# Feature-major products split into two 64-row halves of the array, each half with its own PSUM bank

## The chip, the cores and the metric

The kernel runs on one core of one Trainium2 chip. The core has TensorE (PE, matmuls; PEld, its weight loads), VectorE (DVE), ScalarE (ACT), GpSimd (POOL), and SyncE (SP), whose queue issues most transfers. The metric is the device time of one execution in microseconds, as the median of several runs; lower is better. The median of three runs of the kernel before is 3139.31 us.

## The reference, cut to what matters

Two transformer layers and then one hybrid layer over 256 tokens of width 2048, all in float32. Only two places of it are touched. In each of the two layers the projection of the SSD mixer goes through a causal convolution:

```python
h = rms_norm(x, attn_norm_g[l])
proj = h @ w_in[l]
xbc = jax.nn.silu(causal_depthwise_conv(xbc, conv_w, conv_b))   # xbc: 1536 columns of proj
```

In the hybrid layer two gates of 1024 columns each are taken from the input projection and multiply the outputs of the two attention branches:

```python
ya = (oa * jax.nn.silu(za)) @ w_br_a
yb = (ob * jax.nn.silu(zb)) @ w_br_b
```

The other matmuls (projections, attention, memory attention, the FFN of width 5632) stay as they are.

## The kernel before, in words

Activations and weights are float32, split into a high part that fits the `fp32r` format and a remainder. Each product is three fp32r matmuls, high times high, high times low, low times high, summed in PSUM. Weights come from memory in tiles of 512 KB: SP issues the transfer, ACT writes the high part `wh` (L411), DVE the remainder `wl` (L412). There are five buffers for raw tiles and four for split ones. These three steps have a raised priority, so that they stand early in their engines' orders. The order on PE is the order in which the program is written; on the other engines a scheduler fixes it when the kernel is built, and each engine runs its list in order.

`block` (L414 and on) makes outputs with tokens on the partitions: 512 columns in two PSUM banks, its matmuls being L423, L424 and L425. `block_fm` (L451) makes an output block with features on the partitions, 128 features by 256 tokens: 16 steps over the 2048 inputs, in each of them three matmuls of 128 rows, 128 columns of weights and 256 moving columns (L461, L462, L463), all into one tile of the PSUM pool `psw`. This pool has four banks and serves `block` too.

`block_fm` has two callers. `ssd_conv` calls it 12 times in each of two layers: DVE multiplies the block out of PSUM by the row scale `rb` (L798) into `u`, does the convolution over four taps (L801, L803 three times), ACT takes a tanh (L805) and DVE combines (L806). The tiles `u`, `g` and `th` come from the pool `k1` of six buffers (`t1`). `gate_fm` calls it four times, and is itself called four times in the hybrid layer: ACT takes a tanh out of PSUM (L1303), DVE combines it with the block out of PSUM (L1304). That makes 24 + 16 = 40 blocks.

Between matmuls the program calls `tick()`, which lets waiting tasks emit a step: transposes of earlier results (L377), parts of the attention of other heads (L654 to L670, L1502, L1507), and so on. So the matmuls of such tasks stand between those of a block, in an order that is fixed when the kernel is built. The attention scores of branch A (`scores`, L670) are float32 products of 64 rows, one head on rows 0 to 63, the other on rows 64 to 127, one after the other; a float32 product is two records in the trace.

`early()` raises the priority of what is emitted in it as the weights' steps have it. `HALVES` is `(slice(0, 64), slice(64, 128))`.

Of the kernel before, what the change touches and what calls it, by code (L numbers as in the profile page):

```python
# [14 lines left out]
AF = mybir.ActivationFunctionType  # L15
OP = mybir.AluOpType
# [3 lines left out]
P = 128  # L20
S = 256
# [211 lines left out]
class _Net:  # L233
# [216 lines left out]

    def block_fm(self, pairs, src):  # L451

        nc = self.nc
        pt = self.wbank([P, S])
        for hf in range(2):
            h, l = self.weights(src[hf], 8, P)
            for j in range(8):
                k = hf * 8 + j
                pairs[k // 4] = xh, xl = self.get(pairs[k // 4])
                c = k % 4  # L460
                nc.tensor.matmul(pt, lhsT=h[:, j], rhs=xh[:, c], start=(k == 0), stop=False)  # L461
                nc.tensor.matmul(pt, lhsT=h[:, j], rhs=xl[:, c], start=False, stop=False)  # L462
                nc.tensor.matmul(pt, lhsT=l[:, j], rhs=xh[:, c], start=False, stop=(k == 15))  # L463
                if k in (3, 7, 11):
                    self.tick()
        return pt

# [319 lines left out]
    def ssd_conv(self, l, pairs, rb):  # L789
        nc, I = self.nc, self.I  # L790
        cw = self.small([P, 60], name="cw", bufs=1)
        nc.vector.tensor_scalar(cw, self.p(f"{l}.conv"), 0.5, None, op0=OP.mult)
        cb = [self.slot([P, 4, S], "cb") for _ in range(3)]
        for c in range(12):
            pt = self.block_fm(pairs, I["w_in_x"][l, c])
            u = self.t1([P, 3 + S])
            nc.gpsimd.memset(u[:, 0:3], 0.0)
            nc.vector.tensor_tensor(u[:, 3:], pt, rb, op=OP.mult)  # L798
            w = lambda i: cw[:, c * 5 + i:c * 5 + i + 1]
            g = self.t1([P, S])  # L800
            nc.vector.tensor_scalar(g, u[:, 0:S], w(0), w(4), op0=OP.mult, op1=OP.add)  # L801
            for i in (1, 2, 3):
                nc.vector.scalar_tensor_tensor(g, u[:, i:i + S], w(i), g, op0=OP.mult, op1=OP.add)  # L803
            th = self.t1([P, S])
            nc.scalar.activation(th, g, AF.Tanh)  # L805
            nc.vector.scalar_tensor_tensor(cb[c // 4][:, c % 4], th, 1.0, g, op0=OP.add, op1=OP.mult)  # L806
            if c < 11:
                self.tick()
        return cb
# [486 lines left out]
    def gate_fm(self, pairs, src):  # L1296

        nc = self.nc
        out = self.slot([P, 4, S], "zf")
        for c in range(4):  # L1300
            pt = self.block_fm(pairs, src[c])
            th = self.t1([P, S])
            nc.scalar.activation(th, pt, AF.Tanh, scale=0.5)  # L1303
            nc.vector.scalar_tensor_tensor(out[:, c], th, 1.0, pt, op0=OP.add, op1=OP.mult)  # L1304
            self.tick()
        return out

# [383 lines left out]
```

## Time and profile before

| what | value |
|---|---|
| median of the runs | 3139.31 us (3138.55 to 3139.89, 3 runs) |
| the profiled execution's own time | 3138.04 us |
| its span, first to last instruction | 3136.0 us |
| PE busy | 3114.7 us, 99% |
| DVE busy | 2030.4 us, 65% |
| ACT busy | 1548.2 us, 49% |
| POOL busy | 52.6 us, 2% |
| mean granted TensorE clock | 0.998 of 2.4 GHz |

Busy time of PE counts from the start of a matmul to its modelled end. Matmuls overlap, so the time that one takes of the engine is read from the distance between starts, not from its duration.

### The profile page before, as it was taken

The numbers are of one execution on the slowest core, as the hardware profiler recorded it, in microseconds if no ns is written. First come the engines' busy times: TensorE is split into PE (matmuls) and PEld (weight loads), VectorE is DVE, ScalarE is ACT, GpSimd is POOL, SyncE is SP. The second block draws the span as 40 slices with busy tenths as digits, with TensorE's granted clock in tenths as the row PEclk, the third lists the DMA queues.
The fourth block names the chain that finished last, engine by engine and source line by source line (L and its number), as shares of the span: only waits on it lengthen the run. The fifth ranks groups of instructions, "written<-read, shape, count | busy, mean of one in ns | idle before, by whom it ended". The sixth has DMA issues, their size and how long they took to land.

```text
span 3136.0 us, 42057 instructions
## 1 busy us (share of the span) xinstructions
PE 3114.7 (99%) x15977; PEld 2619.4 (84%) x15977; DVE 2030.4 (65%) x3013; ACT 1548.2 (49%) x2187; POOL 52.6 (2%) x79
## 2 busy tenths in 40 slices
PE   9999999999999999999999999999999999999998
PEld 8988888888888889988888888888878888888887
DVE  6886665555555566886667667777666566455555
ACT  7475564444444455475664444444454456444443
POOL 0010000000000000010000000000000000000000
PEclk9999999999999999999999999999999999999999
DMA  8545555555555555554558777777765543555454
GB/s 299 177 165 168 188 168 188 191 192 191 192 188 192 190 188 177 170 182 151 202 193 288 251 256 273 270 255 260 253 220 191 184 145 123 194 181 182 162 183 152
DMA packets 175162, 625.31 MB, mean 199 GB/s; under 512 B 19696, under 2 KB 19952, under 8 KB 174704
## 3 DMA queue, kind: packets, MB, share of 16 engines
q1 hardware_dynamic: 173952, 620.26, 58.0%
q8 instruction: 125, 2.05, 0.3%
q10 hardware_dynamic: 1008, 2.37, 0.2%
q14 instruction: 77, 0.63, 0.1%
HBM read 620.46 MB, written 2.10 MB: 199 GB/s over the span
## 4 chain that ended last, share of the span: by engine, by line
PE 96%; DVE 1%; DMA 1%; issue 1%; ACT 0%; POOL 0%; SPq 0%; DVEq 0%; POOLq 0%; ACTq 0%
PE pw L423 27%; PE pw L425 27%; PE pw L424 27%; PE pw L461 2%; PE pw L462 2%; PE pw L463 2%; PE mb L377 2%; PE mb L670 1%; DMA wada<-w_ada 0%; DVE wl L412 0%; PE mb L1507 0%; PE mb L909 0%; PE mb L1353 0%; PE mb L892 0%; PE mb L1162 0%
## 5 line engine op out<-in xcount | busy, mean ns | idle before, releaser
L412 DVE TENSOR_TENSOR wl<-raw,wh 128x1024 fp32r<-128x1024 f32 (+3 forms) x1069 | 1285.6, 1204 | 971.7 <-ACT wh L411 969.5
L411 ACT ACTIVATE wh<-raw 128x1024 fp32r<-128x1024 f32 (+3 forms) x1069 | 1114.3, 1043 | 1370.0 <-PE pw L425 1248.5
L423 PE MATMUL pw<-wh,xh 128*128 128x512 f32 (+2 forms) x3952 | 1552.0, 393 | 5.7 <-ACT wh L411 4.6
L425 PE MATMUL pw<-wh,xl 128*128 128x512 f32 (+2 forms) x3952 | 1524.5, 386 | 0.0
L424 PE MATMUL pw<-wl,xh 128*128 128x512 f32 (+2 forms) x3952 | 1523.3, 385 | 0.8 <-DVE wl L412 0.8
L423 PEld LDWEIGHTS pw<-wh,xh 128*128 128x128 f32 x3952 | 743.4, 188 | 151.0 <-ACT wh L411 5.7
L425 PEld LDWEIGHTS pw<-wh,xl 128*128 128x128 f32 x3952 | 742.5, 188 | 150.1 <-DVE xl L368 0.7
L424 PEld LDWEIGHTS pw<-wl,xh 128*128 128x128 f32 x3952 | 743.9, 188 | 142.1 <-DVE wl L412 2.2
L461 PE MATMUL pw<-xh,wh 128*128 128x256 f32 x640 | 183.0, 286 | 0.0
L463 PE MATMUL pw<-xh,wl 128*128 128x256 f32 x640 | 181.0, 283 | 0.0
L462 PE MATMUL pw<-xl,wh 128*128 128x256 f32 x640 | 181.0, 283 | 0.0
L485 DVE TENSOR_TENSOR x<-x,pw 128x512 f32<-128x512 f32 x224 | 145.0, 679 | 3.9 <-PE pw L425 3.9
L1245 DVE CUSTOM_DVE_ANT_0 wada<-wada,crow 128x1024 f32<-128x1024 f32 x96 | 117.3, 1222 | 39.6 <-DMA wada<-w_ada 39.4
L461 PEld LDWEIGHTS pw<-xh,wh 128*128 128x128 f32 x640 | 122.7, 192 | 0.8 <-issue 0.3
L462 PEld LDWEIGHTS pw<-xl,wh 128*128 128x128 f32 x640 | 122.7, 192 | 0.1
L463 PEld LDWEIGHTS pw<-xh,wl 128*128 128x128 f32 x640 | 122.7, 192 | 0.0
L630 ACT ACTIVATE t<-t,mn 128x256 f32<-128x256 f32 (+1 forms) x128 | 57.9, 453 | 44.5 <-DVE mn L627 42.5
L367 ACT ACTIVATE xh<-mb,par 128x256 fp32r<-128x256 f32 x112 | 50.9, 466 | 13.1 <-PE mb L377 12.2
L368 DVE SCALAR_TENSOR_TENSOR xl<-mb,par,xh 128x256 fp32r<-128x256 f32 x112 | 51.9, 478 | 4.0 <-ACT xh L367 2.8
L334 POOL TENSOR_TENSOR xr<-rs,mhalf 128x1 f32<-128x1 f32 x16 | 9.9, 621 | 2482.4 <-DVE rs L330 2278.9
L358 ACT ACTIVATE xh<-mb 128x512 fp32r<-128x512 f32 (+1 forms) x68 | 35.1, 517 | 31.1 <-PE mb L377 16.3
L359 DVE TENSOR_TENSOR xl<-mb,xh 128x512 fp32r<-128x512 f32 (+1 forms) x68 | 39.2, 591 | 4.3 <-ACT xh L358 3.9
(363 smaller groups left out, 1436.0 us busy)
## 6 DMA issues: line engine op xcount, KB each, us to landing
raw<-w_gate SPq DMA_DIRECT2D x176, 512.0 KB, 3.5
raw<-w_up SPq DMA_DIRECT2D x176, 512.0 KB, 3.5
raw<-w_down SPq DMA_DIRECT2D x176, 512.0 KB, 3.5
raw<-w_out SPq DMA_DIRECT2D x96, 512.0 KB, 3.4
wada<-w_ada SPq DMA_DIRECT2D x96, 512.0 KB, 5.6
raw<-w_in_x SPq DMA_DIRECT2D x48, 512.0 KB, 3.8
raw<-w_in_z SPq DMA_DIRECT2D x32, 512.0 KB, 3.5
raw<-w_ma SPq DMA_DIRECT2D x32, 512.0 KB, 3.2
```

Source lines behind the costliest of these rows:

```text
L377: self.nc.tensor.transpose(t[:, j, m * P:(m + 1) * P], src(m), self.ident)
L411: nc.scalar.activation(h, raw, AF.Copy)
L412: nc.vector.tensor_tensor(l, raw, h.bitcast(F32), op=OP.subtract)
L423: nc.tensor.matmul(pt[m], lhsT=xh[:, k, ms], rhs=wh[:, j], start=c == 0, stop=False)
L424: nc.tensor.matmul(pt[m], lhsT=xh[:, k, ms], rhs=wl[:, j], start=False, stop=False)
L425: nc.tensor.matmul(pt[m], lhsT=xl[:, k, ms], rhs=wh[:, j], start=False, stop=c == 4 * n - 1)
L461: nc.tensor.matmul(pt, lhsT=h[:, j], rhs=xh[:, c], start=(k == 0), stop=False)
L462: nc.tensor.matmul(pt, lhsT=h[:, j], rhs=xl[:, c], start=False, stop=False)
L463: nc.tensor.matmul(pt, lhsT=l[:, j], rhs=xh[:, c], start=False, stop=(k == 15))
L485: self.nc.vector.tensor_tensor(xs, xs, pt[m], op=OP.add)
L630: nc.scalar.activation(e[:, a:b], z[:, a:b], AF.Exp, scale=-1.0, bias=mn[:, m:m + 1], accum_out=su[:, m:m + 1])
L1245: nc.vector.tensor_tensor_reduce(out=t, in0=t, in1=self.crow[hf], scale=1.0, scalar=0.0, op0=OP.mult, op1=OP.add, accum_out=self.adap[:, j ...
```

## The change

In `block_fm` each of the three matmuls of a step becomes two, one over rows 0 to 63 of the weights and the moving data, one over rows 64 to 127. They alternate. The first of each two sums into one PSUM tile, the second into another; `block_fm` returns both. A new function `joined` copies the first tile to SBUF on ACT and adds the second to it on DVE, both in `early()`. In `ssd_conv` the multiplication by `rb` then goes from SBUF to SBUF, on POOL instead of DVE. In `gate_fm` the tanh and the combination read the joined block in SBUF instead of PSUM.

```diff
     def block_fm(self, pairs, src):
         nc = self.nc
-        pt = self.wbank([P, S])
+        pt = [self.wbank([P, S]) for _ in range(2)]
         for hf in range(2):
             h, l = self.weights(src[hf], 8, P)
             for j in range(8):
                 k = hf * 8 + j
                 pairs[k // 4] = xh, xl = self.get(pairs[k // 4])
                 c = k % 4
-                nc.tensor.matmul(pt, lhsT=h[:, j], rhs=xh[:, c], start=(k == 0), stop=False)
-                nc.tensor.matmul(pt, lhsT=h[:, j], rhs=xl[:, c], start=False, stop=False)
-                nc.tensor.matmul(pt, lhsT=l[:, j], rhs=xh[:, c], start=False, stop=(k == 15))
+                for i, (w, x) in enumerate(((h, xh), (h, xl), (l, xh))):
+                    for t, b in zip(pt, self.HALVES):
+                        nc.tensor.matmul(t, lhsT=w[b, j], rhs=x[b, c], start=(k == 0 and i == 0),
+                                         stop=(k == 15 and i == 2))
                 if k in (3, 7, 11):
                     self.tick()
         return pt
+
+    def joined(self, pt, out):
+
+        with self.early():
+            self.nc.scalar.activation(out, pt[0], AF.Copy)
+            self.nc.vector.tensor_tensor(out, out, pt[1], op=OP.add)
...
             pt = self.block_fm(pairs, I["w_in_x"][l, c])
             u = self.t1([P, 3 + S])
             nc.gpsimd.memset(u[:, 0:3], 0.0)
-            nc.vector.tensor_tensor(u[:, 3:], pt, rb, op=OP.mult)
+            self.joined(pt, u[:, 3:])
+            nc.gpsimd.tensor_tensor(u[:, 3:], u[:, 3:], rb, op=OP.mult)
...
             pt = self.block_fm(pairs, src[c])
             th = self.t1([P, S])
-            nc.scalar.activation(th, pt, AF.Tanh, scale=0.5)
-            nc.vector.scalar_tensor_tensor(out[:, c], th, 1.0, pt, op0=OP.add, op1=OP.mult)
+            self.joined(pt, out[:, c])
+            nc.scalar.activation(th, out[:, c], AF.Tanh, scale=0.5)
+            nc.vector.scalar_tensor_tensor(out[:, c], th, 1.0, out[:, c], op0=OP.add, op1=OP.mult)
             self.tick()
```

## Rows read from the trace of the kernel before

**Rows 1.** The page: busy time and share of each engine.
```profile
PE 3114.7 (99%) x15977; PEld 2619.4 (84%) x15977; DVE 2030.4 (65%) x3013; ACT 1548.2 (49%) x2187; POOL 52.6 (2%) x79
```
**Rows 2.** The page: the chain that ended last, shares by engine.
```profile
PE 96%; DVE 1%; DMA 1%; issue 1%; ACT 0%; POOL 0%; SPq 0%; DVEq 0%; POOLq 0%; ACTq 0%
```
**Rows 3.** Line L461 from 98 to 128 us: count, durations, first and last start.
```profile
L461 PE MATMUL pw<-xh,wh x84: 283/283/283, 97.9 to 127.8; 128*128 128x256 f32 x84
```
**Rows 4.** Timeline of PE at 61 us: transposes between feature-major products.
```profile
60.94 0.29 PE L463 MATMUL pw<-xh,wl 128*128 128x256 f32 x1
61.06 0.60 PE L377 MATMUL mb<-cst,kva 128*128 128x128 f32 x4
...
61.62 0.28 PE L462 MATMUL pw<-xl,wh 128*128 128x256 f32 x1
```
**Rows 5.** Timeline at 2532 us: 64-row score products between full-array ones.
```profile
2532.04 0.39 PE L424 MATMUL pw<-wl,xh 128*128 128x512 f32 x1
...
2532.27 0.39 PE L425 MATMUL pw<-wh,xl 128*128 128x512 f32 x1
...
2532.59 0.92 PE L670 MATMUL mb<-kt,qt 64*128 64x256 f32 x8
...
2533.44 0.19 PEld L423 LDWEIGHTS pw<-wh,xh 128*128 128x128 f32 x1
...
2533.55 0.19 PEld L424 LDWEIGHTS pw<-wl,xh 128*128 128x128 f32 x1
```
**Rows 6.** Groups on PE, 58.1 to 128.2 us (convolution, first layer).
```profile
L377 PE MATMUL mb<-cst,kva 128*128 128x128 f32 x8 | 1.2, 272 | 0.0
```
**Rows 7.** Groups on PE, 2480.5 to 2531 us (gates, first eight blocks).
```profile
L1438 PE MATMUL mb<-kct,qt 128*64 128x32 f32 x64 | 2.3, 224 | 0.0
L377 PE MATMUL mb<-cst,pc 128*128 128x128 f32 x8 | 1.4, 280 | 0.0
L377 PE MATMUL mb<-cst,ks 128*128 128x128 f32 x4 | 0.6, 272 | 0.0
L1366 PE MATMUL mb<-par,t 128*128 128x64 f32 x4 | 0.6, 260 | 0.0
...
L1425 PE MATMUL mb<-cst,t 128*128 128x128 f32 x1 | 0.3, 273 | 0.0
```
**Rows 8.** Groups on PE, 2632.9 to 2664.4 us (gates, next four blocks).
```profile
L1507 PE MATMUL mb<-t,ks 128*64 128x256 f32 (+1 forms) x32 | 3.0, 332 | 0.0
L656 PE MATMUL mb<-cst,t 128*128 128x128 f32 x8 | 2.2, 272 | 0.0
...
L670 PE MATMUL mb<-kt,qt 64*128 64x256 f32 (+1 forms) x16 | 1.8, 349 | 0.0
```
**Rows 9.** Busy time by stretch: window, its length, then each engine's.
```profile
76.00:82.00 6.00, 6.00 (x52) 6.00 (x52) 6.00 (x19) 2.48 (x4) 0.10 (x1) 1.00 0.66 235
...
118.00:124.00 6.00, 6.00 (x52) 6.00 (x52) 5.14 (x10) 2.43 (x3) 0.10 (x1) 1.00 0.56 182
...
2480.50:2531.00 50.50, 50.49 (x466) 49.95 (x465) 29.88 (x51) 22.49 (x29) 0.00 (x0) 1.00 0.47 165
```
**Rows 10.** Groups on DVE, 58 to 128 us: busy, mean ns, idle before.
```profile
L412 DVE TENSOR_TENSOR wl<-raw,wh 128x1024 fp32r<-128x1024 f32 x26 | 31.7, 1220 | 3.1 <-ACT wh L411 3.1
```
**Rows 11.** Timelines of POOL and of DVE at 228 us.
```profile
228.33 3.00 POOL L1011 TENSOR_TENSOR kv<-kv,rk 128x512 f32<-128x512 f32 x2
...
228.89 1.53 DVE L1013 TENSOR_TENSOR kr<-t,rk 128x512 f32<-128x512 f32 x1
230.35 2.06 DVE L412 TENSOR_TENSOR wl<-raw,wh 128x1024 fp32r<-128x1024 f32 x1
```
**Rows 12.** Line L1303: count, durations, first and last start.
```profile
L1303 ACT ACTIVATE t<-pw x16: 363/366/368, 2487.8 to 2893.3; 128x256 f32<-128x256 f32 x16
```
**Rows 13.** Line L798 over both layers: what ended DVE's idle time before it.
```profile
L798 DVE TENSOR_TENSOR t<-pw,t x24: 414/422/426, 66.2 to 1297.2; 128x256 f32<-128x256 f32 x24
...
  PE pw L463: 3.6, 12
```

## The prediction

> **What bounds the kernel now.** I read the page first, then the chain, then the stretches that the change touches. PE is busy for 99% of the span, DVE for 65%, ACT for 49% [rows 1], and the chain that ended last is 96% PE [rows 2]. So time is won or lost by what a matmul takes of PE, and another engine counts only where it makes PE wait.
>
> What one product takes is the distance between starts: 84 matmuls of L461 start from 97.9 to 127.8 us [rows 3], with one of L462 and one of L463 for each, so 29.9 / (83 x 3) = 120 ns. The 512-column products start 0.23 us apart (the first two of [rows 5]); the 256 columns more cost about 107 ns, so one of 256 columns has some 13 ns on top of its streaming. The trace does not say what these are; they are all that the change can win. Weight loads are busy for 84% of the span while matmuls are busy for 99% [rows 1], so loads already run beside matmuls on the same rows.
>
> **What the change does on PE.** 40 blocks x 48 = 1920 products become 1920 pairs of 64 rows. A pair streams 256 columns on each half. Three questions: do the halves run together, what does a pair take, and what does it cost to change between 128 and 64 rows.
>
> Together: the score products already alternate on the halves. At 2532 us eight records (four of 256 columns, four of 128) take until the next block's load at 2533.44 at most, 0.85 us [rows 5]. A float32 record of 128 columns takes 0.11 us (L463 at 60.94, L462 at 61.62, four transposes and two products of 0.12 between: (0.68 - 0.24) / 4, [rows 4]) and one of 256 twice that. One after the other the eight would take 4 x 0.22 + 4 x 0.11 = 1.32 us; in pairs 0.66. So float32 halves run together. These records stream at half the rate of fp32r (0.22 against 0.107 us for 256 columns), so that fp32r halves do so too is not shown; I take it that they do.
>
> The pair: if each half has its own 107 ns and its own 13 ns, the halves side by side take 120 ns, as one product does now: no gain, no loss. From below, a pair at 107 ns (all 13 hidden) wins 1920 x 13.3 ns = 25.6 us. From above, both records' 13 ns one after the other make 133 ns, a loss of 25.6 us; and halves that don't overlap make 240 ns, a loss of 230 us. I take 120: in the score pairs, the only alternation that the trace has, nothing shows that pairing shortens a record; their time is used up by the streams and the changes of mode, which come next.
>
> The Trainium skill (TensorE: Matmul & The Clock Gate, Part 3, The mechanism) says of packed tiles that each further one adds about 4 ns to the time of one; by it a pair would take 124 ns and the sum below would be 7.7 us higher. The trace's pairs are too coarse here to show 4 ns, and I leave it out.
>
> Changes of mode: L425 at 2532.27 takes 0.23 of PE; the next block's second load, which starts as its first product does, is at 2533.55 [rows 5]. The score group in between took 2533.55 - 2532.27 - 0.23 = 1.05 us, with 0.66 of streams: 0.4 for two changes, 0.2 each. Transposes of 128 rows lose nothing: their 0.11 us [rows 4] is what 128 columns need at that half rate, with no change on either side. Now the feature-major stretches are themselves in 64-row mode, so each group of full-array matmuls inside one costs two changes that were free, and so do a stretch's two ends. Counting groups:
> - convolution: two groups of four transposes [rows 6] and two ends are 6 changes, and the second layer has the same: 12
> - gates, first eight blocks [rows 7]: transposes of `pc` (two groups), of `ks`, L1366 and L1425, one each, are five groups, 10 changes; the two groups of L1438 are already in a mode of their own (64 columns) and change twice either way; ends 2: 12
> - next four [rows 8]: of eight groups L654 to L656 one lies before the stretch and one directly before scores, which leaves six, 12 changes; two groups of L1507 with L1502 ahead of them cost one more each, 2; the scores that stand alone save 2; ends 2: 14
> - last four, nothing between: ends 2.
>
> Sum 40 x 0.2 = 8.0 us. This term rests on measured rows and on the order of PE, which stays as it is.
>
> **What it does on the other engines.** Gates: 16 copies on ACT (0.37 us, by the nearest row, L1303 [rows 12]) and 16 additions on DVE (0.42 by L798 [rows 13], also a 256-column product with a PSUM operand). In the first eight blocks DVE is busy 29.9 and ACT 22.5 of 50.5 us [rows 9], and 8 x 0.8 us fit into the idle time: I cost them at nothing. Without that cover they would be 13 us. A block now takes two of `psw`'s four banks, so a block waits for the one before the last; it has a block's 5.76 us to be copied and added, against some 0.8 us of work.
>
> Convolution is tighter. DVE keeps its count (the addition stands for the product), but at 76 to 82 us of the first layer it is busy 6.00 of 6.00 us, later 5.14 of 6.00 [rows 9], or 4.93 of a block's 5.76. POOL gets a product of 256 columns; the one that it makes of 512 takes 1.5 us [rows 11], so some 0.76. While POOL runs from 228.33 to 231.33, DVE's L412 takes 2.06 us instead of 1.22 and L1013 1.53 [rows 10, 11]: DVE waits for POOL. So a block asks 4.93 + 0.76 = 5.69 of 5.76 us of DVE: it just fits. Two things go on top. DVE's addition waits for ACT's copy, 0.37 us after the point where DVE already waits for PE (3.6 us in 12 waits, 0.30 each [rows 13]); behind it on DVE stand `wl` splits, which PE waits for, and taps. At worst that is 24 x (0.37 - 0.07) = 7 us. And in the first layer, where DVE is full, some four blocks have no room: 4 x 0.76 = 3 us. Against that stand four split weight tiles of two to a block, a lead of up to two blocks. Bounds 0 and 10 us; I take 3, the part that has no slack at all.
>
> **Sum.** From the profiled execution, 3138.04: + 8.0 (changes of mode) + 0 (pairs) + 3 (convolution) = 3149.0. The median of the runs lies 1.27 above that execution, so 3150 us, 0.35% slower. A measurement of this kernel can tell about 0.2%, 6.3 us, from no change.
>
> **Rivals.**
> - The 13 ns vanish, faster: what they are is open, and if they are a cost of loading the rows that are streaming, alternation hides them. At a pair of 115.8 ns it pays the changes of mode (8.0 us / 1920 = 4.2 ns); at 107 to 111 ns it wins 17 to 26 less 8, if the convolution's DVE keeps up: 3122 to 3130. For it: the constant 13 ns. Against: loads already overlap [rows 1], and each half still loads its own rows.
>   The Trainium skill (same page and section) states that loads overlap with running matmuls only when their row groups differ; by that rule this rival holds. The trace agrees only in part: loads overlap on the same rows too.
> - The 13 ns vanish, but DVE, at 5.69 us a block, holds the convolution at its old pace: only the gates' 16 x 48 = 768 pairs win, 7 to 10 us, against 8 + 3 of cost: 3140 to 3143, no change.
> - Both records pay: pairs of 133 ns, 25.6 + 8 + 3: 3176.
> - fp32r halves take turns: 230 + 8, DVE then no bound: 3378. The trace has no fp32r record of 64 rows to exclude it.
> - Pairs as forecast, but DVE or the banks hold the convolution at the upper bound, 8 + 10: 3158.
>
> **How the numbers follow.** Chances: forecast 0.50, with 3144 to 3154; faster rival 0.10; the gain that DVE holds back 0.12; both pay 0.14; turns 0.08; DVE at its bound 0.06. The range leaves out the faster rival and the turns, 0.18: 3136 to 3177. Faster by over 0.2% (below 3133) is the first rival alone, 0.10. Within 0.2% (to 3145.6) lie the held-back gain and the low edge of the forecast, 0.12 + 0.06 = 0.18. The rest is slower, 0.72.
>
> **What would show it.** Starts of pairs in the last gate stretch, where nothing stands between: 120 ns from pair to pair, the stretch as long as before. Gaps of 0.2 us around transposes inside stretches, 40 in all. POOL products of some 0.8 us, and DVE's SBUF operations beside them longer by as much. PE's waits for `wl`, `wh` or DVE in the convolution stay at a few us. The prediction is wrong if pairs start under 116 ns apart, or over 125, or if the change of mode is free between fp32r products.

## The result, and the profile after

The changed kernel takes 3179.74 us (median of 4 runs, 3179.29 to 3180.02) against 3138.93 for the kernel before on the same chip: ratio 1.0132, 95% interval 1.012 to 1.0143. It is slower, as forecast, but by 41 us where 11 were forecast, and just outside the range. The profiled execution's span is 3177.1 us against 3136.0.

The page's busy times (answering to [rows 1]) and the shares of the chain that ended last (to [rows 2]):

```profile
PE 3132.0 (99%) x17897; PEld 2624.1 (83%) x17897; DVE 2042.8 (64%) x3029; ACT 1555.8 (49%) x2227; POOL 67.3 (2%) x103
...
PE 93%; DVE 3%; issue 2%; ACT 1%; DMA 1%; POOL 1%; SPq 0%; DVEq 0%; ACTq 0%; POOLq 0%
```

DVE is busy for no larger share than before, yet it is now 3% of the chain. PE's busy time has grown by 17 us, less than half of the loss: the rest, 24 us, is PE standing still.

Where: the first product of each step, line by line, for the five feature-major stretches of both kernels (two convolutions, three stretches of gates). Columns: count, shortest/median/longest ns, first and last start in us. First the kernel before:

```profile
L461 PE MATMUL pw<-xh,wh x192: 278/283/365, 58.2 to 127.8; 128*128 128x256 f32 x192
L461 PE MATMUL pw<-xh,wh x192: 278/283/365, 1227.0 to 1296.6; 128*128 128x256 f32 x192
L461 PE MATMUL pw<-xh,wh x128: 278/283/385, 2480.5 to 2530.8; 128*128 128x256 f32 x128
L461 PE MATMUL pw<-xh,wh x64: 278/283/387, 2632.9 to 2664.2; 128*128 128x256 f32 x64
L461 PE MATMUL pw<-xh,wh x64: 277/283/283, 2869.2 to 2891.9; 128*128 128x256 f32 x64
```

The same rows of the kernel after:

```profile
L464 PE MATMUL pw<-xh,wh x384: 274/280/412, 58.4 to 142.3; 64*128 64x256 f32 x192
...
L464 PE MATMUL pw<-xh,wh x384: 274/280/384, 1247.7 to 1329.0; 64*128 64x256 f32 x192
...
L464 PE MATMUL pw<-xh,wh x256: 274/280/384, 2517.4 to 2569.3; 64*128 64x256 f32 x128
...
L464 PE MATMUL pw<-xh,wh x128: 275/280/383, 2671.8 to 2705.0; 64*128 64x256 f32 x128
...
L464 PE MATMUL pw<-xh,wh x128: 275/280/381, 2910.4 to 2933.1; 64*128 64x256 f32 x128
```

The lengths go from 69.6, 69.6, 50.3, 31.3, 22.7 to 83.9, 81.3, 51.9, 33.2, 22.7 us. The two convolutions lose 14.3 and 11.7, the gates 1.6, 1.9 and nothing. The distance from the end of a convolution to the next stretch grows as well, from 1099.2 to 1105.4 and from 1183.9 to 1188.4: 6.2 and 4.5. With 0.9 in small pieces that is the whole difference of 41.1 us. 36.7 of it are the convolutions and what follows them directly.

The last gate stretch, where nothing stands between products, is as long as before: a pair takes what one product took. The timeline of PE there (start, duration, both in us; "x2" is a pair):

```profile
2910.35 0.39 PE L464 MATMUL pw<-xh,wh 64*128 64x256 f32 x2
2910.58 0.28 PE L464 MATMUL pw<-xl,wh 64*128 64x256 f32 x2
2910.69 0.28 PE L464 MATMUL pw<-xh,wl 64*128 64x256 f32 x2
2910.81 0.28 PE L464 MATMUL pw<-xh,wh 64*128 64x256 f32 x2
```

Apart from the first, pairs start 0.12 us apart. In the convolution PE waits for other engines. The view of PE's waits (total us, times, longest):

```profile
PE pw L464 <- DVE t L474: 16.4, 19, 1.0
...
PE mb L851 <- DVE y L841: 5.2, 4, 1.7
```

About once a block PE waits until DVE has added the banks of an earlier block (19 times in 24 blocks, 0.9 us each). DVE is late although it is not full. A turn is what DVE does from one block's addition to the next block's. One turn of its list in the second layer (in brackets the idle time before, and what ended it):

```profile
1295.37 0.41 DVE L474 TENSOR_TENSOR t<-t,pw 128x256 f32<-128x256 f32 x1
1296.54 0.41 DVE L810 TENSOR_SCALAR t<-t,cw 128x256 f32<-128x256 f32 x1 [0.75 <-POOL t L805]
1296.98 1.53 DVE L812 SCALAR_TENSOR_TENSOR t<-t,cw,t 128x256 f32<-128x256 f32 x3
1299.05 0.42 DVE L815 SCALAR_TENSOR_TENSOR cb<-t,t 128x256 f32<-128x256 f32 x1 [0.54 <-ACT t L814]
1300.01 2.36 DVE L412 TENSOR_TENSOR wl<-raw,wh 128x1024 fp32r<-128x1024 f32 x2 [0.53 <-ACT wh L411]
1302.28 0.41 DVE L474 TENSOR_TENSOR t<-t,pw 128x256 f32<-128x256 f32 x1
```

A turn takes 6.91 us, where PE needs 48 x 0.12 = 5.76. With one more wait, for ACT's copy, 20 turns that are longer by 1.15 us make 23 of the 26.0 us that the two convolutions lose (an estimate from these rows); some 2 are changes of mode. Of the 6.91, DVE idles 0.75 + 0.54 + 0.53 = 1.82; its work, 5.09, would fit. The three waits are in series with it: POOL's product waits for the addition, the taps for POOL, the tanh on ACT for the taps, the combine for the tanh, the first `wl` for its `wh`. ACT's list has both `wh` behind that tanh, which waits 4.33 us for the taps:

```profile
1298.60 0.42 ACT L814 ACTIVATE t<-t 128x256 f32<-128x256 f32 x1 [4.33 <-DVE t L812]
1298.93 1.99 ACT L411 ACTIVATE wh<-raw 128x1024 fp32r<-128x1024 f32 x2
1300.83 0.36 ACT L473 ACTIVATE t<-pw 128x256 f32<-128x256 f32 x1
```

So both `wl` come after the `wh`, and the next block's addition stands behind both `wl`. The chain closes on itself without PE: addition, POOL, taps, tanh, `wh`, `wl`, addition. A turn of the kernel before, in the same view:

```profile
1269.39 0.48 DVE L803 SCALAR_TENSOR_TENSOR t<-t,cw,t 128x256 f32<-128x256 f32 x1
1269.79 1.22 DVE L412 TENSOR_TENSOR wl<-raw,wh 128x1024 fp32r<-128x1024 f32 x1
1270.92 1.00 DVE L803 SCALAR_TENSOR_TENSOR t<-t,cw,t 128x256 f32<-128x256 f32 x2
1272.31 1.23 DVE L412 TENSOR_TENSOR wl<-raw,wh 128x1024 fp32r<-128x1024 f32 x1 [0.39 <-ACT wh L411]
1273.45 0.42 DVE L806 SCALAR_TENSOR_TENSOR cb<-t,t 128x256 f32<-128x256 f32 x1
1274.17 0.42 DVE L798 TENSOR_TENSOR t<-pw,t 128x256 f32<-128x256 f32 x1 [0.30 <-PE pw L463]
```

There one `wl` stands between the taps, the other ahead of the combine, and the turn ends with a wait for PE.

After the convolution DVE is still behind: PE's L851 waits 5.2 us for it over both layers, and in the first layer the clock falls behind these waits. Windows (length, busy of PE, PEld, DVE, ACT, POOL, granted clock, DMA share, GB/s), the first of them inside the first convolution:

```profile
72.00:78.00 6.00, 4.39 (x43) 4.20 (x45) 5.83 (x22) 2.23 (x5) 0.68 (x2) 0.72 0.26 89
...
160.00:162.00 2.00, 2.00 (x6) 1.58 (x6) 2.00 (x4) 0.38 (x1) 0.00 (x0) 0.50 0.23 45
162.00:164.00 2.00, 2.00 (x8) 1.56 (x7) 1.77 (x5) 1.06 (x1) 0.00 (x0) 0.71 0.57 223
```

At 0.50, the 1.2 GHz level, the 512-column products start 0.43 us apart instead of 0.23. The second layer's waits were as long, but the clock stayed at 1.00; some 3.4 us at half the clock lose 1.7, which is the difference of 6.2 against 4.5 us. Inside the first convolution the clock fell as well, behind two waits of 0.9 us, but it is not what makes that stretch long: the kernel of whole rows in the same order, below, has 1.00 throughout both convolutions and needs 83.3 and 81.2 us.

### The profile page after: what moved, and what is told of

Read it like the earlier page. It is cut to its first block, busy times and chain, and to the rows that moved or that the text cites. A ratio compares the mean times of both kernels' runs of the same rounds, so it can differ in the third digit from the quotient of the medians.

```text
span 3177.1 us, 45982 instructions
## 1 busy us (share of the span) xinstructions
PE 3132.0 (99%) x17897; PEld 2624.1 (83%) x17897; DVE 2042.8 (64%) x3029; ACT 1555.8 (49%) x2227; POOL 67.3 (2%) x103
## 4 chain that ended last, share of the span: by engine, by line
PE 93%; DVE 3%; issue 2%; ACT 1%; DMA 1%; POOL 1%; SPq 0%; DVEq 0%; ACTq 0%; POOLq 0%
PE pw L423 27%; PE pw L425 27%; PE pw L424 27%; PE pw L464 5%; PE mb L377 2%; DVE wl L412 1%; PE mb L678 1%; ACT wh L411 1%; PE mb L1517 0%; PE mb L1363 0%; PE mb L918 0%; DVE t L474 0%; PE mb L901 0%; PE mb L662 0%; PE mb L1171 0%
## 5 line engine op out<-in xcount | busy, mean ns | idle before, releaser
L464 PE MATMUL pw<-xh,wh 64*128 64x256 f32 x1280 | 215.1, 287 | 17.3 <-DVE t L474 16.4
L464 PE MATMUL pw<-xl,wh 64*128 64x256 f32 x1280 | 209.9, 282 | 0.0
L464 PE MATMUL pw<-xh,wl 64*128 64x256 f32 x1280 | 207.7, 281 | 0.0
L464 PEld LDWEIGHTS pw<-xh,wh 64*128 64x128 f32 x1280 | 161.0, 188 | 25.6 <-DVE t L474 20.5
L464 PEld LDWEIGHTS pw<-xh,wl 64*128 64x128 f32 x1280 | 159.8, 189 | 0.0
L464 PEld LDWEIGHTS pw<-xl,wh 64*128 64x128 f32 x1280 | 159.6, 189 | 0.0
L814 ACT ACTIVATE t<-t 128x256 f32<-128x256 f32 x24 | 10.0, 418 | 103.1 <-DVE t L812 99.3
L368 DVE SCALAR_TENSOR_TENSOR xl<-mb,par,xh 128x256 fp32r<-128x256 f32 x112 | 51.8, 478 | 4.2 <-ACT xh L367 3.0
```

The source lines that it names most:

```text
L368: nc.vector.scalar_tensor_tensor(l[:, i], src[:, i], gain[:, i:i + 1], h[:, i].bitcast(F32), op0=OP.mult, op1=OP.subtract)
L464: nc.tensor.matmul(t, lhsT=w[b, j], rhs=x[b, c], start=(k == 0 and i == 0), stop=(k == 15 and i == 2))
```

## The experiments

Each time stands beside runs of the kernel before on the same chip (medians 3137.93 for the first four, 3137.99 for the next four, 3138.23 us for the last two). "Stretches" are first to last start of the high-by-high products, as above; before they were 69.6, 69.6, 50.3, 31.3, 22.7.

**Halves in the gates alone.** The convolution is as in the kernel before.

```diff
-            pt = self.block_fm(pairs, I["w_in_x"][l, c])
+            pt = self.block_whole(pairs, I["w_in_x"][l, c])   # block_fm of before
...
-            self.joined(pt, u[:, 3:])
-            nc.gpsimd.tensor_tensor(u[:, 3:], u[:, 3:], rb, op=OP.mult)
+            nc.vector.tensor_tensor(u[:, 3:], pt, rb, op=OP.mult)
```

> The split stays in the gates (16 of 40 blocks); the convolution is as in the kernel before. Ring theory (in the convolution ACT, DVE and POOL wait for one another in a fixed order, one turn per block, 6.9 us instead of 5.76): the two convolution stretches return to 69.8 us each, and what stays is the gates' changes of mode, 3.6 us inside their stretches and about 1 at the ends: 3143 to 3145 us. Split theory (the 64-row products themselves cost PE time, in proportion to the blocks): 16/40 of 41, about 3155 us.

3142.65 us, ratio 1.0014 (1.0004 to 1.0023). Stretches 69.6, 69.6, 51.9, 33.2, 22.8: those of the gates are as long as in the kernel after. The halves cost about 4.7 us there, so what is lost beyond that belongs to the convolution.

**Whole rows, two banks.** Copy, addition and POOL are kept, products have 128 rows; steps 0 to 7 go into one bank, 8 to 15 into the other.

```diff
-                    for t, b in zip(pt, self.HALVES):
-                        nc.tensor.matmul(t, lhsT=w[b, j], rhs=x[b, c], start=(k == 0 and i == 0),
-                                         stop=(k == 15 and i == 2))
+                    nc.tensor.matmul(pt[hf], lhsT=w[:, j], rhs=x[:, c], start=(j == 0 and i == 0),
+                                     stop=(j == 7 and i == 2))
```

> Products of 128 rows again, but the first eight steps of a block sum into one bank and the last eight into the other, so that the copy, the addition and POOL's product stay as in the changed kernel; no change of mode. Ring theory: the convolution still takes 6.8 to 6.9 us a block, the total is that of the changed kernel less some 6 us of mode changes, 3171 to 3176 us. Split theory: 3139 to 3145 us.

3143.69 us, ratio 1.0019 (1.0009 to 1.0028); stretches 70.7, 69.6, 51.8, 31.2, 22.7. (The 51.8 of the first gates has another cause than in the kernels with halves: transposes there wait 1.3 us for DVE's `pc`, which they do not do in the kernel after.) The theory that the joining (ACT's copy of one bank and DVE's addition of the other) itself makes the chain fell: the joining is all here, and the turn is 5.76 us. What differs is the order of DVE's list, where a `wl` is between the taps again and the combine stands behind the next addition. But a bank is also complete half a block early here, so the order was not yet shown to be the cause.

**The rms product back on DVE.** `nc.gpsimd.tensor_tensor` becomes `nc.vector.tensor_tensor`, nothing else.

> The changed kernel with the product by the row scale on DVE instead of POOL. Ring theory: a turn loses DVE's wait for POOL (0.76 us) and gains a DVE product (0.42), 6.9 becomes about 6.55 us a block, 24 x 0.35 = 8 us less: 3168 to 3174 us. Lock theory (POOL's product holds the port that it shares with DVE, and this is the cost): the convolution returns to 5.8 us a block, 3145 to 3150 us.

3175.2 us, ratio 1.0117 (1.0102 to 1.0132); stretches 82.1, 79.6. A turn is 6.72 us (additions at 1284.43 and 1291.15), not the 6.55 expected: from addition to taps it is 0.98 us where it was 1.17. DVE stalled by POOL's use of SBUF is not the cause; the same chain with another link is nearly as long.

**Taps emitted a block later.** Taps, tanh and combine of block c are written behind the joining of block c+1.

> The changed kernel, but the taps, the tanh and the combination of a convolution block are emitted after the next block's joining, so that DVE has them to do while ACT and POOL work on the next block. Same instructions. Ring theory: DVE's waits for POOL and ACT (1.8 us of a turn of 6.9) are filled, a block takes 5.76 to 5.9 us: 3146 to 3153 us. Load theory (DVE's work with the addition, about 5.1 us a block, and the lock are too much in themselves): above 3165 us.

3178.89 us, ratio 1.013 (1.0115 to 1.0145). The scheduler put DVE's list into the same order all the same, and the turn is 6.91. This told nothing about the theories, except that the order in which the code is written does not settle the order of the list. The theory from here on: the time goes to the order of DVE's and ACT's lists, and halves, banks and hops only come with it. The next three runs force or free that order.

**Halves, with the order mended.** Dependencies without a semaphore put the tanh of block c behind the copy of block c+1, and the combine behind its addition; both also get the raised priority.

```diff
+        def gate(c, g, copied=None, added=None):
+            th = self.t1([P, S])
+            with self.tc.issue_after(copied) if copied else self.early():
+                nc.scalar.activation(th, g, AF.Tanh)
+            with self.tc.issue_after(added) if added else self.early():
+                nc.vector.scalar_tensor_tensor(cb[c // 4][:, c % 4], th, 1.0, g, op0=OP.add, op1=OP.mult)
...
+            if late:
+                with self.early():
+                    gate(*late, *ins)      # ins: copy and addition of this block
```

> The kernel after, with every product still two of 64 rows; only in the convolution the tanh of block c stands behind the joined copy of block c+1 on ACT, and its combine behind the addition of block c+1 on DVE, so that the list of DVE reads addition, combine of the block before, four taps, two wl, and that of ACT copy, tanh of the block before, two wh. Theory (the order of the two lists makes a chain addition, POOL, taps, tanh, combine, wh, wl, addition of 6.9 us a block): without tanh and combine in the chain the turn falls to PE's 5.76 us or a little over it, the convolutions to 70 to 72 us each, and the time to 3143 to 3150 us. Rival (the halves themselves, or banks filled to the end of the block, keep the turn at 6.9): convolutions stay at 80 us or more, time 3170 us or more.

3150.2 us, ratio 1.0038 (1.0023 to 1.0053); stretches 72.8, 70.9, 51.9, 33.2, 22.8. DVE's list in the second layer:

```profile
1266.28 0.41 DVE L474 TENSOR_TENSOR t<-t,pw 128x256 f32<-128x256 f32 x1
1266.62 0.42 DVE L808 SCALAR_TENSOR_TENSOR cb<-t,t 128x256 f32<-128x256 f32 x1
1267.57 0.41 DVE L822 TENSOR_SCALAR t<-t,cw 128x256 f32<-128x256 f32 x1 [0.54 <-POOL t L814]
1268.02 1.52 DVE L824 SCALAR_TENSOR_TENSOR t<-t,cw,t 128x256 f32<-128x256 f32 x3
1269.46 2.35 DVE L412 TENSOR_TENSOR wl<-raw,wh 128x1024 fp32r<-128x1024 f32 x2
1271.73 0.41 DVE L474 TENSOR_TENSOR t<-t,pw 128x256 f32<-128x256 f32 x1
```

The same instructions turn in 5.45 us (DVE is catching up here, and could keep PE's 5.76): the waits for tanh and `wh` are gone. PE's waits for L474 fall from 16.4 to 1.9 us. What was lost after the convolutions is gone too (1099.8 and 1184.7 us to the next stretch, against 1105.4 and 1188.4 after). 29 of the 41 us come back with the order alone.

**Whole rows, both banks filled to the end.** Products of 128 rows go to the two banks in turn; lists free.

```diff
-                    for t, b in zip(pt, self.HALVES):
-                        nc.tensor.matmul(t, lhsT=w[b, j], rhs=x[b, c], start=(k == 0 and i == 0),
-                                         stop=(k == 15 and i == 2))
+                    q = k * 3 + i
+                    nc.tensor.matmul(pt[q % 2], lhsT=w[:, j], rhs=x[:, c], start=(q < 2), stop=(q >= 46))
```

> Products of all 128 rows, one after another into the two banks in turn, so that both banks are filled until the end of the block as in the kernel after; copy, addition and product on POOL as there. The scheduler is left free, and its lists come out with the combine behind the next addition and a wl between the taps. Theory of the order: 5.76 us a block, convolutions 70 to 71 us, time 3141 to 3146 us, as with the first half of the block in one bank. Rival (a bank finished half a block early was what made that kernel fast): convolutions 75 us or more each, 3155 us or more.

3145.05 us, ratio 1.0022 (1.0013 to 1.0032); stretches 71.4, 69.6, 51.7, 31.2, 22.7. The early bank was not what made the other kernel of whole rows fast.

**The same, with the order of the kernel after.** `wh` and `wl` of block c+2 are held behind the tanh and the combine of block c.

```diff
+        with self.behind(0):       # issue_after(tanh of block c)
             nc.scalar.activation(h, raw, AF.Copy)
+        with self.behind(1):       # issue_after(combine of block c)
             nc.vector.tensor_tensor(l, raw, h.bitcast(F32), op=OP.subtract)
```

> The same products of 128 rows as in whole_alternating, but in the convolution the wh and wl of block c+2 are held behind the tanh and the combine of block c, so that the lists of ACT and DVE read as in the kernel after: addition, taps, combine, two wl; copy, tanh, two wh. Theory of the order: the turn is 6.9 us a block without a single product of 64 rows, convolutions 80 to 84 us each, time 3165 to 3178 us. Rival (the halves are what costs): 70 to 72 us each, 3141 to 3147 us.

3165.38 us, ratio 1.0087 (1.0071 to 1.0102); stretches 83.3, 81.2, 51.6, 31.2, 22.6. DVE's turn, without one product of 64 rows:

```profile
1284.93 0.41 DVE L481 TENSOR_TENSOR t<-t,pw 128x256 f32<-128x256 f32 x1
1286.10 0.41 DVE L820 TENSOR_SCALAR t<-t,cw 128x256 f32<-128x256 f32 x1 [0.76 <-POOL t L815]
...
1288.62 0.43 DVE L825 SCALAR_TENSOR_TENSOR cb<-t,t 128x256 f32<-128x256 f32 x1 [0.55 <-ACT t L824]
1289.57 2.36 DVE L415 TENSOR_TENSOR wl<-raw,wh 128x1024 fp32r<-128x1024 f32 x2 [0.52 <-ACT wh L413]
1291.85 0.42 DVE L481 TENSOR_TENSOR t<-t,pw 128x256 f32<-128x256 f32 x1
```

6.92 us, with the three waits of the kernel after. The stretches of the convolution are as long as there. PE's own wait is another, though: 15.2 us in 20 waits for `wl`, not for the banks; DVE's turn sets the pace in both. Only the loss behind the convolutions is missing. The weights for what follows were not held, and in the second layer three `wl` run ahead of the taps from 1319.84 us on; DVE's first `y` (L841 of the kernel after) then starts 7.6 us behind the last step of the convolution instead of 12.9.

**Three lower halves, then three upper.**

```diff
-                for i, (w, x) in enumerate(((h, xh), (h, xl), (l, xh))):
-                    for t, b in zip(pt, self.HALVES):
+                for t, b in zip(pt, self.HALVES):
+                    for i, (w, x) in enumerate(((h, xh), (h, xl), (l, xh))):
```

> The kernel after with the six products of a step in another order: three on the lower rows, then three on the upper. If neighbours on different halves run together and those on one half do not, only one lower and one upper product meet at each change of half: four places of 120 ns a step in place of three, 7.68 us a block against 5.76. Over 40 blocks that is 77 us where PE sets the pace; the convolutions, at 6.9 us a block in the kernel after, would go to 92 us each, the gates by 1.92 us a block, and the time to 3210 to 3230 us. If the alternation has no part in it (both halves overlap in any order), the time stays at about 3140 to 3180 us; if halves never run together as in the rival of 120 ns each, it is near 3378 us.

3175.78 us (one run); stretches 82.0, 79.0, 51.9, 33.3, 22.8. The gates are as long as with alternating halves, though the program lists a half's three products first. The timeline of PE from the first product of the last stretch:

```profile
2907.20 0.39 PE L464 MATMUL pw<-xh,wh 64*128 64x256 f32 x2
2907.42 0.29 PE L464 MATMUL pw<-xl,wh 64*128 64x256 f32 x2
2907.53 0.29 PE L464 MATMUL pw<-xh,wl 64*128 64x256 f32 x2
```

From the first product on, two with the same operand names start together. So the alternation gains nothing in the gates: an upper product starts beside a lower one that is three places ahead of it in the list.

**The kernel before, with the order of the kernel after.** The same holding of `wh` and `wl`, in the kernel of one bank and no hops.

> The kernel before (whole rows, one bank, the product with rms straight from the bank on DVE), with wh and wl of block c+2 held behind the tanh and the combine of block c, so that DVE's list reads product, taps, combine, two wl. In the kernel after the same list with POOL in it turns in 6.91 us, 0.76 of which DVE waits for POOL. If the chain is a plain sum of its links, the turn without that hop is about 6.15 us: 0.39 over PE's 5.76, 4.7 us for each convolution of twelve blocks, time 3143 to 3150 us. If only the chain with the POOL hop is long enough to bind, or the order is not what costs, 3137 to 3140 us.

3151.4 us, ratio 1.0044 (1.0029 to 1.0059); stretches 77.7, 74.6, 50.3. The order costs the kernel before 13 us by itself; PE waits there for `wl`, 5.2 us in 16 waits. A turn is 6.28 us by DVE's products with the row scale, 0.52 over PE's, where a plain sum of links gave 6.15; so copy, addition and POOL account for 0.63 of the 6.91.

```profile
1280.55 0.42 DVE L809 TENSOR_TENSOR t<-pw,t 128x256 f32<-128x256 f32 x1
...
1286.83 0.42 DVE L809 TENSOR_TENSOR t<-pw,t 128x256 f32<-128x256 f32 x1
```

Over the kernel before, the joining with free lists costs 7 us (whole rows, both banks filled to the end), the order without the joining 13, and both together 27 (whole rows in the order of the kernel after): 7 more than the sum.

**Hops alone.** One bank, whole rows, no addition; ACT copies the bank and POOL multiplies by rms; lists free.

```diff
-            nc.vector.tensor_tensor(u[:, 3:], pt, rb, op=OP.mult)
+            with self.early():
+                nc.scalar.activation(u[:, 3:], pt, AF.Copy)
+            nc.gpsimd.tensor_tensor(u[:, 3:], u[:, 3:], rb, op=OP.mult)
```

> The kernel before with whole rows in one bank; in the convolution alone ACT copies the bank early and POOL multiplies by rms, where DVE did it straight from the bank; no second bank, no addition; the lists free. If only the order costs, and the scheduler keeps a wl between the taps here, the hops cost nothing that lasts: convolutions 69.8 to 71 us, time 3137 to 3142 us. If the hop through POOL costs DVE its port or its time, 0.3 us or more a block would stand on PE: 3146 us or more.

3137.86 us, ratio 1.0 (0.999 to 1.0009); stretches 69.6, 69.6, 50.3, 31.2, 22.7. The rms product on POOL and the copy on ACT cost nothing by themselves.

## Why the prediction was wrong

**Pairs: right.** Halves of fp32r products run together, and a pair takes 0.12 us, neither 0.107 nor 0.133. The last gate stretch keeps its 22.7 us. The rivals of vanishing 13 ns, of 133 ns and of halves in turn are out. The 4 ns a pair that the Trainium skill (TensorE: Matmul & The Clock Gate, Part 3, The mechanism) led to are not seen: the second record starts 3 to 4 ns after the first, but the next pair comes 120 ns after the last.

**Changes of mode: right, a little large.** The group of L1366 in the gates, halves (the kernel with halves in the gates alone):

```profile
2486.31 0.28 PE L481 MATMUL pw<-xh,wl 64*128 64x256 f32 x2
2486.52 0.66 PE L1392 MATMUL mb<-par,t 128*128 128x64 f32 x4
2487.11 0.39 PE L481 MATMUL pw<-xh,wh 64*128 64x256 f32 x2
2487.33 0.28 PE L481 MATMUL pw<-xl,wh 64*128 64x256 f32 x2
```

From the last pair ahead of it to the second one behind it are 1.02 us. In the kernel before the same takes 0.68:

```profile
2484.70 0.28 PE L463 MATMUL pw<-xh,wl 128*128 128x256 f32 x1
2484.82 0.55 PE L1366 MATMUL mb<-par,t 128*128 128x64 f32 x4
2485.18 0.36 PE L461 MATMUL pw<-xh,wh 128*128 128x256 f32 x1
2485.38 0.28 PE L462 MATMUL pw<-xl,wh 128*128 128x256 f32 x1
```

So two changes cost 0.34, 0.17 each against the 0.2 forecast: 40 of them would be 6.8 us instead of 8.0. The gates' stretches lengthened by 3.5 us and the distances between them by 0.6, where 5.6 stood for their 28 changes.

**Convolution: the step that failed.** The prediction took 3 us, with bounds of 0 and 10, and measured were 26.0 in the stretches (some 2 of them changes of mode) and 10.7 behind them. It weighed DVE's load, 4.93 us and 0.76 of waiting for POOL against a block's 5.76, and concluded that it just fits. The load does fit (5.09 us). But that sum supposed that DVE's list stays as it was, with its waits beside other work. A scheduler makes the lists when the kernel is built, and with the new instructions it put both `wh` and both `wl` behind tanh and combine. Then 1.82 us of waits lie in series with the load. That order alone makes the kernel before 13 us slower; with the joining it takes kernels of whole rows to the same 83 and 81 us; undone in the kernel of halves, it leaves 3150.2 us. That this is the time forecast is in part chance: of the 12 us over the kernel before some 7 are changes of mode, where 8 were forecast, and 5 other things, where 3 were. The named mechanism of the high bound, ACT's copy delaying DVE's addition, is no link of the chain: in the turn above the copy ends at 1301.19, and the addition starts at 1302.28, behind both `wl`.

The rival of DVE or the banks holding the convolution had the right place and PE's waits show it as described, but its price was that of the upper bound, 10 us, under a third of the 35 that came. (With its terms its time is 3157, not 3158.)

**POOL.** Forecast were products of some 0.8 us, with DVE waiting as long for SBUF. In the kernel after they take 0.638 us in the median, while DVE stands idle for their data; where DVE works beside them they grow instead: median 1.405 us with the hops alone, with DVE's `wl` beside it at 1.23 us, its usual time. The 0.75 us a turn for which DVE stands before the taps come close to the 0.76 forecast by luck: they are a wait for POOL's data, which lies in series, and not DVE instructions that run longer beside POOL.

**What stays open.** Why the scheduler orders the lists one way for 64-row products and another for the same work with 128-row ones was not found; only that it does, and what the order costs. In the kernel with halves in the gates alone the distance from the second convolution to the gates is longer by 1.5 us: 0.3 of it arise at 1837 us, 0.2 at 2350, and the rest right behind, at a granted clock of 0.50, which lasted 6.8 us against 3.4 in the kernel before; why it lasted longer is open. No version here beats the kernel before: a pair gains nothing, and the changes of mode remain.

## What to carry to other kernels

When an edit touches instructions on engines whose order a scheduler makes, the load per block says only whether the work can fit; add up the chain from an instruction back to itself one block later, waits included, and compare that with the pace of the bound engine. If a changed kernel is slow with no engine busier than before, compare the order of the lists, and force another before blaming the operations. Splitting a product over the row halves gained nothing here, where each half streams the same 256 columns as the whole did (0.12 us a pair, 0.12 a product), and each excursion to full-array products cost two changes.

## What was unexpected in the hardware

- Products on the two row halves need not alternate in the list: with three lower ones ahead of three upper ones they still ran in pairs 0.12 us apart, from the first product of a stretch. The records of a pair then start 10 ns apart, with three places of the list between them, instead of 3 to 4 ns with one; that fits a list run as written, which no view shows directly. The Trainium skill (TensorE: Matmul & The Clock Gate, Part 3, The mechanism) states that matmuls start and end in the order of the program. With the list as written the trace does not agree: in that order the first upper product could start no sooner than the third lower one, a step would take four places of 0.12 us, and the last stretch of 64 steps 30 us (an estimate from these rows); it kept 22.8.
- By the lines on L1366 above, the 0.34 us of two changes lie in three places: 0.09 from the last pair to the group (0.21 against 0.12), 0.23 from the group's start to the first pair behind it (0.59 against 0.36), 0.02 in the step after that (0.22 against 0.20). The 0.22 us behind a first pair are thus no sign of the mode; behind a wait of PE, too, a first product of 128 rows is followed after 0.22 us (1290.85 and 1291.07 in the kernel of whole rows in the order of the kernel after).
- The same waits of PE for L841, after either convolution (2.6 us in each layer), were followed by a granted clock of 0.50 for some 3 us in the first layer and of 1.00 in the second. With the taps emitted a block later, and waits of 2.5 and 2.6 us, the clock fell behind both.
- A POOL product of 256 columns took 0.638 us alone and 1.41 us beside a `wl` of DVE that had started 0.31 us earlier, and that `wl` was not lengthened; in [rows 10, 11] it was DVE's `wl` that took longer beside POOL.
